# Gate slabs 2, 4 and 6 in halves over neighbouring pairs of heads, and three orders made fixed, in a two-layer decoder trunk

## The chip, the core and the metric

The kernel runs on one core of one Trainium2 chip. The time is device microseconds of one execution; the number that is compared is the median of several executions. A matrix engine (PE, with its weight loads shown apart as PEld), a vector engine (DVE), an activation engine (ACT), a general engine (POOL) and a queue engine that issues the transfers (SP) run beside each other, each through its own list of instructions in order, and wait for each other on semaphores.

## The reference

Two layers over 1024 tokens of width 1024. Each computes one input projection with the columns [main | memory queries | main gate | memory gate], then a main branch and a cross-attention of four heads into 256 memory tokens, and then the output projection and a layer norm.

```
h = x @ w_in
y = concat([main(u_main) * silu(g_main), memory(q_mem) * silu(g_mem)])
x = layer_norm(alpha * x + y @ w_out)
```

Layer 0's main branch is a causal pooling. Layer 1's is the part that the change touches, attention of 16 heads of 64 channels with forget gates; k, v and cum come from one shared projection of layer 1's input:

```
logits[t, s] = q_t . k_s / 8 + cum[t] - cum[s]      (s <= t)
out = softmax(logits) @ v
```

Everything is in float32. The kernel splits each float32 operand of a product into a high and a low part and adds three products (high·high, high·low, low·high).

## The kernel before

Nearly all matrix work comes in slabs. A slab (`slab`, L169) is 128 output channels by 1024 tokens: 48 products of 512 columns, in two weight pieces of 256 KB; for each piece come 12 products for tokens 0 to 511 and then 12 for tokens 512 to 1023. A piece is loaded through SP into a tile `raw` (4 buffers) and split into two tiles `w` (6 buffers); in the attention of layer 1 POOL does that split (`gp_hi_lo`, L144 and L145), elsewhere ACT and DVE (`hi_lo`, L140 and L141). When a 512-token half is complete it is taken out of the accumulator (`pj`, 3 banks): a gate by ACT L192 and DVE L193, keys by L645 and L646, queries by L656 and L657, values by an ACT copy (L669) and then `values_of`, which halves them to 16 bit and has them transposed by SP.

The stage of the change is `fox` (L781). It goes through the 16 heads in order, two heads to a pair, and in each head through 8 steps i = 0..7, one for each tile of 128 queries, the longest (tile 7, 1024 keys) first. A step on tile i of a head has these parts:

- `probs` (L692): POOL masks the diagonal block of the row tile R (L702); the mask of a tile writes what the previous tile's maximum read, so it follows that maximum. PE multiplies queries by keys in one or two parts of up to 512 keys (L167, into `L`, 2 banks). DVE adds R and takes the running minimum of the negated logits in one instruction for each part (L709); that frees the bank. ACT takes the exponentials into `T` with their sums (L715).
- `halves` of the tile before, called by `behind` between the last maximum and the exponentials in program order: DVE adds the sums (L726 or L728) and inverts them (L729); ACT scales to a 16-bit high half (L732), DVE gives the low half (L733).
- `turn` (L742): SP transposes both halves.
- `values` (L746), five steps later (LAG): PE multiplies by the values (L167, into `O`, 1 bank), ACT and DVE take it out into `o` (L758, L759). `pair_out` multiplies `o` by the pair's gate on POOL (L768) and stores it to y1d.

Between these, `Fill.pump` hands PE products of slabs that are needed later: the fills. Each pair of heads spreads its own fills evenly over its 16 steps, 0.4 of a step's share ahead of the values and 0.6 behind them. During pair p the fills hold the keys, queries and values of pair p+1 (three slabs, none of them in pair 7), and gates: 0 and 1 in pair 0, 2 in pair 2, 4 in pair 4, 7 in pair 7. Gates 3, 5 and 6 are fills of pair 7 too, as `late_gate`: the stored pair is read back from y1d into an `R` buffer (2 in all), multiplied on POOL (L778) and stored again. So the pairs 0 to 7 have 3, 3, 4, 3, 4, 3, 3 and 4 slabs.

In pair 7 the first 8 of 24 pieces of W_out are also loaded (`OutProj.fetch`, L350) and split on ACT and DVE (`OutProj.split`, through `hi_lo`), and two pieces of the memory branch's output (`OutProj.early`). Five more steps follow the last head (`hd == HEADS`), with the output projection's first 48 products as fill, and then `OutProj.rest`, the projection and the norm.

PE is under `manual_schedule`: its order is the program's. On the other engines and on SP a scheduler places the instructions ahead of time by its own model of when their inputs are ready, with the program order as priority, so an instruction can be placed ahead of others that come before it in the program. At run time every engine keeps the placed order.

Of the kernel before, what the change touches and what calls it, by code (L numbers as in the profile page):

```python
# [18 lines left out]
P = 128  # L19
S = 1024  # L20
# [51 lines left out]
def trunk_kernel(ctx, tc, x, xT, memT, win, wk, wv0, wv, wmk, wmv, wout, poolw, pscale, lng, lnb, bforget, out):  # L72
# [65 lines left out]
    def hi_lo(hi, lo, src):  # L138

        nc.scalar.copy(hi, src)  # L140
        nc.vector.tensor_tensor(lo, src, hi.bitcast(F32), ALU.subtract)  # L141
# [27 lines left out]
    def slab(pieces_dram, XH, XL, evac, banks=("pj", 3)):  # L169

        accs = [ps([P, NH], *banks) for _ in range(2)]
        for pc in range(2):
            ready = isinstance(pieces_dram, list)
            h, l = pieces_dram[pc] if ready else split_w(pieces_dram[pc], [P, 4, P])
            for n in range(2):
                for k in range(4):
                    kt = pc * 4 + k
                    for i, (a, b) in enumerate(((h, XH), (h, XL), (l, XH))):
                        nc.tensor.matmul(  # L179
                            accs[n], a[:, k, :], b[:, kt, n * NH : (n + 1) * NH],  # L180
                            start=kt == 0 and i == 0, stop=kt == KT - 1 and i == 2,
                        )
# [76 lines left out]
    def gate_units(w_dram, dst, XH, XL):  # L259
        return slab(w_dram, XH, XL, lambda cols, acc: gate(acc, dst[:, cols]))  # L260
# [75 lines left out]
    class OutProj:  # L336
# [16 lines left out]
        def split(self, upto):  # L353

            while self.n < upto:
                self.fetch(self.n + 1)
                n = self.n
                kk, nh, j = self.KKS[n // 4], n // 2 % 2, n % 2
                if j == 0:
                    self.ws[nh][kk] = self.wtile(n // 2)  # L360
                h, lo = self.ws[nh][kk]
                hi_lo(h[j], lo[j], self.raws.pop(0))
                self.n += 1
# [18 lines left out]
        def early(self, yh, yl):  # L382


            for j in range(2):
                r, two = raw([P, 2, 2 * P]), slice(2 * j, 2 * j + 2)
                nc.sync.dma_start(r, self.yd[2, :, two, : 2 * P])
                yield
                hi_lo(yh[:, two, :], yl[:, two, :], r)
# [146 lines left out]
    with tc.tile_pool(name="in1", bufs=1) as in1:  # L536
# [101 lines left out]
        def qk_units(p):  # L638
# [12 lines left out]
            yield from slab(wk[p], XH, XL, k_evac)  # L651
            qs = [xy() for _ in range(2)]
# [9 lines left out]
            pairs[p] = list(zip(qs, ks, ws))  # L662

        def pair_units(p):

            yield from qk_units(p)
            if p >= 2:
                u = MK([P, S], F32)
                yield from slab(wv[p - 2], XH, XL, lambda cols, acc: nc.scalar.copy(u[:, cols], acc))  # L669
            pairs[p].append(first_vs[p] if p < 2 else values_of(u))  # L670
# [15 lines left out]

        def forget_rows(hd):
# [4 lines left out]
        def probs(hd, i, R, sums, behind):  # L692
# [9 lines left out]
            nc.gpsimd.affine_select(R[:, qs], R[:, qs], [[-1, P]], ALU.is_ge, -NEG, base=0, channel_multiplier=1)  # L702
# [3 lines left out]
            for n, (lo, up) in enumerate(parts):  # L706
# [3 lines left out]
                top = m[:, n : n + 1]  # L710
            behind()
# [9 lines left out]
        def halves(hd, i, es, sums):  # L721

            L, r = (i + 1) * P, tiny(1)
            one, two = (sums[:, n, hd % 2, i : i + 1] for n in range(2))
            if len(es) == 2:
# [3 lines left out]
            nc.vector.reciprocal(r, r)  # L729
            pair = sb([P, 2 * S], "P", 4, F16)  # L730
# [50 lines left out]
        def fox(following, out_proj):  # L781
# [3 lines left out]
            def gate_ahead(pr):  # L785
                gs[pr] = G()
                fill.add(gate_units(win[1, 12 + pr], gs[pr], XH, XL), SLAB)

            ahead_R = forget_rows(0)
            for hd in range(HEADS + 1):  # L790
# [3 lines left out]
                if hd < HEADS:  # L794
                    if b == 0:
# [3 lines left out]
                        for ahead in {0: (0, 1), 2: (2,), 4: (4,), 7: (7,)}.get(pr, ()):  # L799
                            gate_ahead(ahead)  # L800
                            if ahead == 0:
                                fill.add(following, SLAB)
                        for late in (3, 5, 6) if pr == 7 else ():
                            fill.add(late_gate(late), SLAB)
                    R, ahead_R = ahead_R, None
                for i in range(ST if hd < HEADS else LAG):
# [3 lines left out]
                    new, split = None, []  # L810

# [7 lines left out]
                    if pr == 7:  # L819
                        step = b * ST + i  # L820
                        if step == 7:
                            lead = out_proj.early(*(xy((P, 4, 2 * P)) for _ in range(2)))
                        if step in (7, 9, 10, 12):
                            next(lead)
                        out_proj.split(min(step - 1, 6) if step < 14 else step - 7)
                        out_proj.fetch(min(step + 1, 6) if step < 12 else min(step - 5, 8))
                    if hd < HEADS:
                        new = (hd, tile_of, o)
                        fresh[0] = probs(hd, tile_of, R, sums, behind)
                    else:  # L830
                        behind()
                    fill.pump(part * FRAC[0])
# [82 lines left out]
```

## Time and profile before

| what | value |
|---|---|
| median of 3 runs | 1272.26 us (1271.57 to 1277.35) |
| profiled execution, its own time | 1275.16 us |
| its span, first to last instruction | 1273.4 us |
| granted PE clock, mean | 0.997 |
| DMA moved | 178.66 MB |

The profile is of one execution. Busy times are of one engine; an engine can be busy for several instructions at once, since they overlap in its pipeline. The number behind an x counts instructions. In a timeline row stand the start, the duration, engine, line and operation, out<-in by tile names, and in brackets how long the engine was idle ahead of it and on whom it waited. A row of the waits gives the total, the number of waits and the longest one.

### The profile page before, as it was taken

The page shows a single profiled execution, that of the slowest core. Times are in us where ns is not written, and L with a number is a line of the kernel's source. Part 1 is how long each engine was busy: PE and PEld are TensorE (multiplying, and loading weights), DVE is VectorE, ACT ScalarE, POOL GpSimd, SP SyncE. Part 2 cuts the span into 40 slices and gives each one's busy share as a digit, 9 for nine tenths or more (in the row PEclk, how much of TensorE's full clock was granted, in tenths as well). Part 3 has the DMA queues.
Part 4 walks back from the last instruction along what each step waited for, and adds up shares of the span by engine and source line. Part 5 has one row for each costly group of instructions (what it writes and reads, how often), then busy time and mean ns, then how long its engine had stood idle before and what let it go on. Part 6 is the DMA issues. An engine that isn't in the chain of part 4 may idle for free. (4 is left out here: it accounts for less than half of the span.)

```text
span 1273.4 us, 19681 instructions
## 1 busy us (share of the span) xinstructions
PE 1243.5 (98%) x7018; PEld 1032.7 (81%) x7018; DVE 803.8 (63%) x1901; ACT 578.5 (45%) x1273; POOL 174.2 (14%) x276
## 2 busy tenths in 40 slices
PE   9999999999999999999999999999999999899997
PEld 6888888888888888888887778887887777777885
DVE  6444766376455555377456878777877887664644
ACT  5233643242321123266225777666667677652110
POOL 0000000000000000000013334342333323430000
PEclk9999999999999999999999999999999999999999
DMA  6333444232553324244516786867877687884430
GB/s 224 108 100 100 117 117 132 83 119 89 158 197 100 106 84 134 75 116 115 162 51 180 137 184 155 195 157 175 187 160 178 157 196 171 209 224 149 166 115 34
DMA packets 267427, 178.66 MB, mean 140 GB/s; under 512 B 212288, under 2 KB 225728, under 8 KB 267328
## 3 DMA queue, kind: packets, MB, share of 16 engines
q1 hardware_dynamic: 267328, 177.40, 52.3%
q8 instruction: 55, 0.90, 0.3%
q14 instruction: 44, 0.36, 0.1%
HBM read 94.97 MB, written 22.61 MB: 92 GB/s over the span
## 5 line engine op out<-in xcount | busy, mean ns | idle before, releaser
L179 PE MATMUL pj<-A,w 128*128 128x512 f32 x2928 | 723.4, 395 | 0.8 <-ACT A L140 0.8
L179 PEld LDWEIGHTS pj<-A,w 128*128 128x128 f32 x2928 | 536.5, 188 | 103.9 <-ACT A L140 2.4
L141 DVE TENSOR_TENSOR w<-raw,w 128x512 fp32r<-128x512 f32 x106 | 74.0, 700 | 105.9 <-ACT w L140 105.1
L715 ACT ACTIVATE T<-MK,s 128x512 f32<-128x512 f32 x192 | 110.8, 577 | 53.1 <-DVE s L709 39.6
L140 ACT CAST w<-raw 128x512 fp32r<-128x512 f32 x106 | 65.7, 621 | 149.8 <-PE pj L179 103.0
L733 DVE SCALAR_TENSOR_TENSOR P<-T,s,P 128x512 f16<-128x512 f32 x192 | 111.5, 613 | 29.8 <-ACT P L732 27.6
L732 ACT ACTIVATE P<-T,s 128x512 f16<-128x512 f32 x192 | 102.7, 576 | 45.5 <-issue 17.2
L167 PE MATMUL L<-B,B 128*128 128x512 f32 (+3 forms) x384 | 92.0, 344 | 14.5 <-DVE s L709 14.1
L167 PEld LDWEIGHTS L<-B,B 128*128 128x128 f32 x384 | 69.8, 188 | 36.8 <-DVE s L709 23.9
L619 POOL MEMSET G<- 128x128 f32 x1 | 0.2, 205 | 610.2 <-DVE V L333 610.2
L709 DVE CUSTOM_DVE_ANT_0 MK<-L,R 128x512 f32<-128x512 f32 (+3 forms) x128 | 72.9, 570 | 12.0 <-PE L L167 7.2
L167 PEld LDWEIGHTS <-V 128*128 128x128 f16 x1152 | 65.2, 99 | 18.6 <-issue 18.6
L167 PE MATMUL O<-T,V 128*128 128x128 f16 x1152 | 76.2, 221 | 1.1 <-DVE G L759 1.1
L141 DVE TENSOR_TENSOR T<-T,T 128x1024 fp32r<-128x1024 f32 x23 | 28.1, 1223 | 70.2 <-PE L L376 51.3
L145 POOL TENSOR_TENSOR w<-raw,w 128x512 fp32r<-128x512 f32 x54 | 70.6, 1307 | 3.8
L140 ACT CAST T<-T 128x1024 fp32r<-128x1024 f32 x23 | 24.2, 1050 | 98.4 <-DMA T<-y0d 50.6
L702 POOL TENSOR_SCALAR_AFFINE_SELECT R<-R 128x128 f32<-128x128 f32 x128 | 42.7, 336 | 180.4 <-DVE s L709 99.2
L144 POOL TENSOR_SCALAR w<-raw 128x512 fp32r<-128x512 f32 x54 | 35.8, 664 | 139.9 <-PE pj L179 131.3
L212 PE MATMUL pj<-T,w 128*128 128x256 f32 x384 | 48.7, 284 | 0.9 <-DVE w L141 0.8
L212 PEld LDWEIGHTS pj<-T,w 128*128 128x128 f32 x384 | 47.6, 192 | 2.0 <-DVE w L141 1.3
L376 PE MATMUL pj<-B,T 128*128 128x512 f32 x186 | 46.5, 392 | 0.5 <-DVE T L141 0.5
L376 PE MATMUL L<-B,T 128*128 128x512 f32 x174 | 43.0, 391 | 0.0
(214 smaller groups left out, 1598.1 us busy)
## 6 DMA issues: line engine op xcount, KB each, us to landing
raw<-in_win_dram SPq DMA_DIRECT2D x96, 256.0 KB, 2.8
raw<-in_wout_dram SPq DMA_DIRECT2D x48, 256.0 KB, 2.9
B<-B SPq DMA_DIRECT2D x32, 256.0 KB, 4.0
R<-cumd SPq DMA_DIRECT2D x16, 512.0 KB, 4.3
y0d<-Y SPq DMA_DIRECT2D x12, 512.0 KB, 3.1
T<-y0d SPq DMA_DIRECT2D x12, 512.0 KB, 3.9
T<-y1d SPq DMA_DIRECT2D x11, 512.0 KB, 4.3
raw<-in_wmk_dram SPq DMA_DIRECT2D x16, 256.0 KB, 2.6
```

The lines of the kernel that those rows point to most:

```text
L140: nc.scalar.copy(hi, src)
L141: nc.vector.tensor_tensor(lo, src, hi.bitcast(F32), ALU.subtract)
L145: nc.gpsimd.tensor_tensor(lo, src, hi.bitcast(F32), ALU.subtract)
L167: nc.tensor.matmul(acc, a, b, start=i == 0, stop=i == len(terms) - 1)
L179: nc.tensor.matmul(accs[n], a[:, k, :], b[:, kt, n * NH : (n + 1) * NH], start=kt == 0 and i == 0, stop=kt == KT - 1 and i == 2,)
L212: nc.tensor.matmul(acc, w[:, k, :], m[pc][:, k, :], start=pc == 0 and k == 0 and i == 0, stop=pc == 1 and k == 3 and i == 2,)
L376: nc.tensor.matmul(accs[a][nh], y[:, k, a * P : (a + 1) * P], w, start=kt == 8 and i == 0, stop=kt == 7 and i == 2,)
L702: nc.gpsimd.affine_select(R[:, qs], R[:, qs], [[-1, P]], ALU.is_ge, -NEG, base=0, channel_multiplier=1)
L709: nc.vector.tensor_tensor_reduce(p[:, lo:up], lg, R[:, lo:up], 1.0, top, ALU.add, ALU.min, m[:, n : n + 1])
L715: nc.scalar.activation(e, p[:, lo:up], AF.Exp, bias=top, scale=-1.0, accum_out=sums[:, n, hd % 2, i : i + 1],)
L732: nc.scalar.activation(pair[:, lo:up], e, AF.Copy, scale=r)
L733: nc.vector.scalar_tensor_tensor(pair[:, L + lo : L + up], e, r, pair[:, lo:up], ALU.mult, ALU.subtract)
```

## The change

Five things are done.

1. `slab` and `gate_units` take `ns`, the 512-token halves that they compute. Gate pr for the pairs 2, 4 and 6 is computed as half 0 at the end of pair pr−1's fills and half 1 at the end of pair pr's. A half loads and splits both weight pieces of its gate again. Gate 1 is in halves too, both in pair 0, ahead of and behind pair 1's remaining slab. Gate 6 is no longer a late gate. The pairs 0 to 7 then have 3, 3.5, 3.5, 3.5, 3.5, 3.5, 3.5 and 3 slabs.
2. Within a pair's fills the order is keys, values, queries (before: keys, queries, values). The half gate comes behind them. `values_of` is called behind the queries.
3. `inverse_of` (the two small DVE instructions of L726 to L729) stands in the program behind the first part of the next tile's maximum, ahead of the second; `halves` keeps the rest.
4. Each mask is placed behind the mask before it on POOL (`issue_after`).
5. The splits of W_out in `fox` and of `early` are pinned behind what precedes them in the program on ACT and on DVE (`keep_in_program_order`). They stand behind `probs` of their step rather than ahead of it, and their steps and those of the loads are given by two lists. The splits in `rest` are not pinned.

```diff
     def hi_lo(hi, lo, src, pinned=False):
+        pin = tc.keep_in_program_order if pinned else lambda ins: ins
+        pin(nc.scalar.copy(hi, src))
+        pin(nc.vector.tensor_tensor(lo, src, hi.bitcast(F32), ALU.subtract))
...
-    def slab(pieces_dram, XH, XL, evac, banks=("pj", 3)):
-        accs = [ps([P, NH], *banks) for _ in range(2)]
+    def slab(pieces_dram, XH, XL, evac, banks=("pj", 3), ns=(0, 1)):
+        accs = {n: ps([P, NH], *banks) for n in ns}
...
-            for n in range(2):
+            for n in ns:
...
+            yield from slab(wk[p], XH, XL, k_evac)
+            if p >= 2:
+                u = MK([P, S], F32)
+                yield from slab(wv[p - 2], XH, XL, lambda cols, acc: nc.scalar.copy(u[:, cols], acc))
             qs = [xy() for _ in range(2)]
...
             yield from slab(win[1, p], XH, XL, q_evac)
+            pairs[p] = [*zip(qs, ks, ws), first_vs[p] if p < 2 else values_of(u)]
...
+            with tc.issue_after(masked[-1]) if masked else nullcontext():
+                masked.append(
+                    nc.gpsimd.affine_select(R[:, qs], R[:, qs], [[-1, P]], ALU.is_ge, -NEG, base=0, channel_multiplier=1).ins
+                )
...
                 top = m[:, n : n + 1]
+                if n == 0:
+                    inverse()
             behind()
...
-            def gate_ahead(pr):
-                gs[pr] = G()
-                fill.add(gate_units(win[1, 12 + pr], gs[pr], XH, XL), SLAB)
+            def gate_ahead(pr, ns):
+                if pr not in gs:
+                    gs[pr] = G()
+                fill.add(gate_units(win[1, 12 + pr], gs[pr], XH, XL, ns), len(ns) * SLAB // 2)
...
-                        for ahead in {0: (0, 1), 2: (2,), 4: (4,), 7: (7,)}.get(pr, ()):
-                            gate_ahead(ahead)
-                            if ahead == 0:
-                                fill.add(following, SLAB)
-                        for late in (3, 5, 6) if pr == 7 else ():
+                        if pr == 0:
+                            gate_ahead(0, (0, 1))
+                            gate_ahead(1, (0,))
+                            fill.add(following, SLAB)
+                            gate_ahead(1, (1,))
+                        elif pr == 7:
+                            gate_ahead(7, (0, 1))
+                        else:
+                            gate_ahead(pr + pr % 2, (1 - pr % 2,))
+                        for late in (3, 5) if pr == 7 else ():
                             fill.add(late_gate(late), SLAB)
...
                     if pr == 7:
                         step = b * ST + i
-                        if step == 7:
+                        out_proj.fetch((0, 0, 1, 2, 3, 4, 5, 6, 6, 6, 7, 7, 7, 8, 8, 8)[step])
+                        if step == 9:
                             lead = out_proj.early(*(xy((P, 4, 2 * P)) for _ in range(2)))
-                        if step in (7, 9, 10, 12):
+                        if step in (9, 12):
                             next(lead)
-                        out_proj.split(min(step - 1, 6) if step < 14 else step - 7)
-                        out_proj.fetch(min(step + 1, 6) if step < 12 else min(step - 5, 8))
...
+                    if pr == 7:
+                        out_proj.split((0, 0, 0, 1, 2, 3, 4, 5, 6, 6, 6, 6, 7, 7, 8, 8)[step], True)
+                        if step in (11, 15):
+                            next(lead)
```

More of the change, by code (lines that the diff above doesn't have):

```diff
@@ L1 @@
-from contextlib import ExitStack
+from contextlib import ExitStack, nullcontext
 from itertools import islice
@@ L257, in transposes, with gate_units @@
         since[0] = 0
-    def gate_units(w_dram, dst, XH, XL):
-        return slab(w_dram, XH, XL, lambda cols, acc: gate(acc, dst[:, cols]))
+    def gate_units(w_dram, dst, XH, XL, ns=(0, 1)):
+        return slab(w_dram, XH, XL, lambda cols, acc: gate(acc, dst[:, cols]), ns=ns)
     def mem_attention(l, XH, XL, kv, qtile, ytile, yd):
@@ L351, in fetch, with split @@
                 self.raws.append(r)
-        def split(self, upto):
+        def split(self, upto, pinned=False):
             while self.n < upto:
@@ L685, in start_units @@
             yield from islice(following, 30)
+        masked = []
         def forget_rows(hd):
@@ L690, in forget_rows, with probs @@
             return R
-        def probs(hd, i, R, sums, behind):
+        def probs(hd, i, R, sums, inverse, behind):
             q, kx, ky = pairs[hd // 2][hd % 2]
@@ L729, in halves @@
             nc.vector.reciprocal(r, r)
+            return r
+        def halves(hd, i, es, r):
+            L = (i + 1) * P
             pair = sb([P, 2 * S], "P", 4, F16)
```

31 lines of the change are left out of this document (13 added, 18 removed).

## The prediction

> **What bounds the kernel now.** I read the page first, for the engines' shares.
>
> ```profile
> span 1273.4 us, 19681 instructions
> ...
> PE 1243.5 (98%) x7018; PEld 1032.7 (81%) x7018; DVE 803.8 (63%) x1901; ACT 578.5 (45%) x1273; POOL 174.2 (14%) x276
> ```
>
> PE is busy 98% of the span, and the change takes no product away: the same slabs are computed, in another order. So only time in which PE stands, or runs slowly, can be won. Next came the windows, cut where the first query-key product of each pair of heads stands in the timeline (pairs 0 to 7, then the five last steps with the beginning of the output projection).
>
> ```profile
> core 0: us, PE busy (x) PEld busy (x) DVE busy (x) ACT busy (x) POOL busy (x), PEclk, DMA share, GB/s
> 672.70:723.40 50.70, 48.78 (x295) 39.50 (x295) 39.72 (x116) 35.27 (x85) 17.02 (x30) 1.00 0.75 167
> 723.40:776.40 53.00, 51.24 (x337) 41.58 (x337) 41.36 (x121) 37.54 (x90) 18.91 (x32) 1.00 0.75 172
> 776.40:837.60 61.20, 61.20 (x385) 50.86 (x385) 47.72 (x138) 41.67 (x95) 23.44 (x35) 1.00 0.76 175
> 837.60:890.30 52.70, 51.09 (x337) 41.60 (x337) 40.88 (x118) 37.28 (x89) 18.83 (x32) 1.00 0.74 169
> 890.30:951.60 61.30, 61.30 (x387) 50.93 (x385) 47.71 (x138) 41.66 (x95) 21.27 (x32) 1.00 0.79 171
> 951.60:1004.10 52.50, 51.07 (x337) 41.63 (x336) 40.89 (x118) 37.28 (x89) 18.83 (x32) 1.00 0.77 173
> 1004.10:1057.10 53.00, 51.37 (x337) 41.53 (x336) 43.42 (x127) 38.90 (x91) 16.94 (x28) 1.00 0.79 180
> 1057.10:1124.60 67.50, 61.39 (x374) 49.46 (x372) 48.44 (x133) 43.14 (x98) 25.37 (x36) 0.97 0.83 195
> 1124.60:1155.80 31.20, 28.57 (x154) 22.32 (x152) 19.17 (x28) 13.73 (x24) 7.64 (x8) 1.00 0.79 259
> ```
>
> The columns are length, then busy time of PE, PEld, DVE, ACT and POOL. Pairs 2 and 4, with four slabs, are full: PE is busy from end to end. The three-slab pairs 1, 3, 5 and 6 are not. What a slab costs is seen where PE runs undisturbed, in the chain of waits:
>
> ```profile
> 1166.59 5.44 PE pj L376 x24
> ```
>
> 24 products of 512 columns take 5.44 us, so a slab of 48 takes 10.9. A four-slab pair is longer by only 61.25 − 52.8 = 8.45 us. The lighter pairs thus lose 2.4 us each, and pair 7, with four slabs and 67.5 us, loses over 6. The waits say of whom:
>
> ```profile
> PE L L167 <- DVE s L709: 14.1, 15, 3.1
> POOL R L702 <- DMA R<-cumd: 45.2, 11, 8.8
> DVE P L733 <- ACT P L732: 27.6, 58, 1.1
> DVE s L726 <- ACT T L715: 21.6, 18, 4.9
> POOL w L144 <- PE pj L179: 131.3, 37, 47.8
> ```
>
> PE stands 14.1 us in all for a bank of logits that the maximum (L709) has not read yet. The timeline of pair 1's second head shows why the maximum is late there:
>
> ```profile
> 756.22 0.73 PE L167 MATMUL L<-B,B 128*128 128x512 f32 x2 [0.22 <-DVE s L709]
> 757.41 0.51 PE L167 MATMUL L<-B,B 128*128 128x256 f32 x2 [0.46 <-DVE s L709]
> 759.02 0.54 POOL L702 TENSOR_SCALAR_AFFINE_SELECT R<-R 128x128 f32<-128x128 f32 x2 [6.66 <-DMA R<-cumd]
> 759.60 0.48 DVE L709 CUSTOM_DVE_ANT_0 MK<-L,R,s 128x256 f32<-128x256 f32 x1 [0.80 <-POOL R L702]
> 764.59 0.73 PE L167 MATMUL L<-B,B 128*128 128x512 f32 x2 [1.08 <-DVE s L709]
> ```
>
> POOL holds two masks. The first is the next head's and waits 6.66 us for its row to land; the second is the one that the running head needs, queued behind it. When it comes, DVE has stood 0.80 us, and PE stands 0.22 + 0.46 + 1.08 = 1.76 us. In pair 7 it is something else:
>
> ```profile
> 1076.03 0.73 PE L167 MATMUL L<-B,B 128*128 128x512 f32 x2 [2.39 <-DVE s L709]
> ...
> 1097.89 2.81 POOL L778 TENSOR_TENSOR R<-R,G 128x256 f32<-128x256 f32 x4 [4.92 <-DMA R<-y1d]
> 1098.41 1.32 ACT L140 CAST B<-raw 128x512 fp32r<-128x512 f32 x2 [3.87 <-DMA raw<-in_wout_dram]
> 1101.18 0.21 DVE L726 TENSOR_SCALAR s<-sums 128x1 f32<-128x1 f32 x1 [4.88 <-ACT T L715]
> 1102.82 0.73 PE L167 MATMUL L<-B,B 128*128 128x512 f32 x2 [3.11 <-DVE s L709]
> ...
> 1104.90:1108.40 3.50, 3.50 (x20) 2.73 (x19) 2.65 (x9) 2.35 (x6) 1.59 (x3) 0.51 0.99 212
> ```
>
> Two W_out casts stand ahead of the exponentials on ACT and wait 3.87 us for their pieces; four products of a late gate stand ahead of a mask on POOL. DVE then waits 4.88 us for the sums and PE 3.11. The last row, a window, shows the granted clock at 0.51 for 3.5 us just after: another 1.7 us lost.
>
> **The change part by part.** *Half gates, the order of masks, pairs 1 to 6.* Today these six take 53.0 + 61.2 + 52.7 + 61.3 + 52.5 + 53.0 = 333.7 us with 20 slabs. After, they hold 21, gate 6's slab coming from pair 7, so like for like today is 333.7 + 10.9 = 344.6. Two roads give the length of a pair with 3.5 slabs. From a full one, half a slab less: 61.25 − 5.44 = 55.8. From a light one, without the mask's stall, half a slab more: 52.8 − 1.76 + 5.44 = 56.5. I take 56.1: 336.6, a gain of 8.0 us. The ends are 55.8 (gain 9.8) and a pair that goes on losing what the light ones lose, 52.8 + 5.44 = 58.24 (loss 4.8). DVE's 47.7 busy us in a full pair, 41 to 43 in a light one, fit under 56.
>
> *What the halves add.* Eight more weight pieces to load and to split on POOL; away go one read and one store of 512 KB, and four products L778, for which four L768 come.
>
> ```profile
> L145 POOL TENSOR_TENSOR w<-raw,w 128x512 fp32r<-128x512 f32 x54 | 70.6, 1307 | 3.8
> L144 POOL TENSOR_SCALAR w<-raw 128x512 fp32r<-128x512 f32 x54 | 35.8, 664 | 139.9 <-PE pj L179 131.3 <-DMA raw<-in_win_dram 8.5
> ```
>
> A split is 0.66 + 1.31 = 1.97 us, so POOL gets 15.8 us more over six pairs, where it is busy 17 to 23 of 53 to 61. In a half slab each piece feeds 12 products, 2.72 us at the least, and POOL mostly waits for PE to free a buffer (131.3 us). I cost it at nothing; if a late transfer holds POOL, a mask or PE's weights come late by that wait, at most what the 4.92 us shows.
>
> *Queries last.* The next pair's first product needs them. Their last half is complete 24 products ahead of the pair's end, 5.4 us with other steps' products between, and is taken out by two of these on DVE behind two on ACT:
>
> ```profile
> L657 DVE SCALAR_TENSOR_TENSOR B<-pj,B 64x512 fp32r<-64x512 f32 x32 | 22.0, 689 | 2.2 <-ACT B L656 1.3
> ```
>
> That is some 2 us on each engine, and the half gate covers it. Without that cover each pair would begin up to 2 us late. The values' raw tile is kept through the queries' slab: one of four `MK` buffers, of which the maxima need two at a time. Both at nothing.
>
> *The inverse inside the maximum.* It lets ACT begin the high half one part (0.6 us) sooner; today DVE waits 27.6 us for ACT's L732, 58 times. Against it: the 18 waits for the sums (21.6 us, 1.2 each) may come to stand ahead of the second part, and behind them wait that part, the bank that it frees and PE. For pairs 1 to 6 both ends lie within those above; I add nothing there.
>
> *Pair 7.* It gives a slab away: 67.5 − 10.9 = 56.6 like for like. If the pinned casts and the ordered masks end the stalls, 3.11 + 2.39 + 1.7 = 7.2 us go: 49.4. DVE doesn't allow that:
>
> ```profile
> L193 DVE SCALAR_TENSOR_TENSOR G<-G,pj 128x512 f32<-128x512 f32 x32 | 21.9, 684 | 7.1 <-ACT G L192 6.3
> raw<-in_wout_dram SPq DMA_DIRECT2D x8, 256.0 KB, 4.1
> ```
>
> Its 48.4 busy us lose one gate, 2 × 0.68, and are 47.0. In the last light pair DVE was not busy for 53.0 − 43.4 = 9.6 us, 1.8 of them the mask's stall: 47.0 + 7.8 = 54.8. The earlier inverse takes at most 27.6 / 8 = 3.4 us of that: 51.4. I take the middle, 53.1, a gain of 3.5; the ends are none and 7.2. The pins add a wait that the trace does not show: a pinned cast stops ACT until its piece has landed, and behind it stand the next high half, the values' first copy and the next exponentials; on DVE the pinned difference holds the low half and the next maximum. A piece is asked for in a step and cast behind the exponentials of the next one, 3.3 us (53 / 16) or more later; it lands after 4.1 us in the median of pair 7 (the second row). So short waits are likely and long ones are not; up to 1 us each hides in ACT's idle time (42 busy of 53).
>
> [...]
>
> *The five last steps.* `rest` keeps its unpinned splits. PE is idle 31.2 − 28.6 = 2.6 us there; I take no change, and ±2.6 as ends.
>
> *The sum.* 8.0 + 3.5 = 11.5 us less. The profiled execution took 1275.16 us (span 1273.4 and what lies around it) and would take 1263.7; the median of the three runs lies 2.9 us lower, so the forecast is 1272.26 − 11.5 = 1260.8. Its own range is 1252.7 (9.8 + 7.2 + 2.6 less) to 1265.9.
>
> **The rivals.** *DVE becomes the bound in every pair.* The inverse's waits land inside the maximum and pairs 1 to 6 stay as lossy as light ones: +4.8 − 3.5 = +1.3, so 1273.6, no change. For it: DVE at 41 to 43 of 53 us. Against it: pairs 2 and 4 ran full with the same work on DVE per head. 0.12.
>
> *The pinned casts stop ACT (slower).* Ten casts in pair 7 with a wait of w each take 10w, of which 11 us hide in ACT's idle time. From w = 2.3 us this eats the whole gain; at 3 us, below the 3.87 seen above, it costs 30 − 11 = 19 us: 1279.8. For it: 4.1 us to land against a step of 3.3, on a queue that also issues the transposes in order. Against it: the casts come a step later than the loads. 0.13.
>
> *POOL and DVE hold each other up.* Some rows of the same operation:
>
> ```profile
> L141 DVE TENSOR_TENSOR B<-raw,B 128x512 fp32r<-128x512 f32 x6 | 5.6, 949 | 0.0
> L141 DVE TENSOR_TENSOR w<-raw,w 128x512 fp32r<-128x512 f32 x106 | 74.0, 700 | 105.9 <-ACT w L140 105.1
> ```
>
> The first is of pair 7, with POOL at work, and takes 949 ns instead of 700. If the eight new splits held DVE for half of their 15.8 us, 7.9 of the 11.5 would go: 1268.7, no change. Against it: L657 and L193, which read one operand from an accumulator, keep 689 and 684 ns in the same stage. 0.06. [...]
>
> *It doesn't do what it says in pair 7.* A pin fixes only what precedes a cast in the program, and late gates 3 and 5 still read through R. Pair 7 wins nothing: 1272.26 − 8.0 = 1264.3. 0.11.
>
> **How the numbers follow.** The forecast has the remaining 0.58. A measurement of this kernel can tell about 0.5% from no change: 6.4 us, so faster is below 1265.9 and slower above 1278.6. Faster: 0.57 + 0.10 of the last rival = 0.67. Slower: 0.13 of the casts and 0.02 for their mixture with the others = 0.15. The rest, 0.18, is no change. The range goes from the forecast's low end, 1252.7, up over the DVE rival to 1274.0; it leaves out the casts' case and a little on either side, under 0.2.
>
> **What would show it.** Right: the masks' wait for R (45.2 us, 11 times) nearly gone, with none queued ahead of a running head's; pairs 1 to 6 at 56 us each with PE idle under 0.5; pair 7 near 53 without a window at half clock; PE's 14.1 us for L709 below 5. Wrong: pairs at 58, with L726 ahead of a second L709 in DVE's waits; or ACT's casts waiting over 2 us for W_out in pair 7 with PE standing behind L709; or L141 and L247 stretched beside L145.

## The result, and the profile after

| | before | after |
|---|---|---|
| median of 8 runs | 1276.15 us (1271.57 to 1281.69) | 1283.06 us (1279.83 to 1285.36) |
| profiled execution, its span | 1273.4 us | 1280.5 us |

The ratio is 1.0048 (95% interval 1.0029 to 1.0067): slower by half a per cent, where 11.5 us less was forecast. From the page of the changed kernel:

```profile
span 1280.5 us, 19721 instructions
...
PE 1245.0 (97%) x7018; PEld 1036.3 (81%) x7018; DVE 808.1 (63%) x1901; ACT 580.3 (45%) x1273; POOL 185.3 (14%) x292
```

The work is the same and the shares have hardly moved; the stages tell more. Windows of the changed kernel, cut at the same products as before (pairs 0 to 7, the last steps, and two short stretches of pair 7); the last three columns are the granted clock, the DMA share and GB/s:

```profile
core 0: us, PE busy (x) PEld busy (x) DVE busy (x) ACT busy (x) POOL busy (x), PEclk, DMA share, GB/s
671.40:721.00 49.60, 48.25 (x295) 39.69 (x295) 38.70 (x115) 34.55 (x83) 20.63 (x34) 1.00 0.74 175
721.00:777.50 56.50, 56.14 (x362) 46.37 (x362) 43.77 (x123) 39.71 (x92) 22.28 (x37) 1.00 0.75 170
777.50:835.00 57.50, 56.28 (x361) 46.20 (x360) 44.90 (x129) 39.55 (x92) 23.07 (x36) 1.00 0.88 175
835.00:892.30 57.30, 56.13 (x362) 46.36 (x361) 45.45 (x129) 39.78 (x92) 23.19 (x37) 1.00 0.86 175
...
1006.80:1063.90 57.10, 56.04 (x361) 46.33 (x360) 45.29 (x129) 39.78 (x92) 20.21 (x32) 1.00 0.79 176
1063.90:1132.20 68.30, 54.92 (x327) 43.14 (x327) 45.72 (x131) 41.54 (x98) 18.38 (x31) 0.88 0.72 171
1132.20:1163.40 31.20, 27.97 (x153) 22.36 (x152) 19.34 (x29) 13.86 (x25) 8.23 (x8) 1.00 0.78 243
1088.40:1095.20 6.80, 6.09 (x28) 4.74 (x28) 3.72 (x9) 2.46 (x6) 1.45 (x3) 0.50 1.05 211
1119.10:1129.40 10.30, 5.42 (x14) 3.60 (x15) 3.81 (x12) 5.06 (x13) 2.18 (x3) 0.50 0.84 200
```

Pairs 1 to 6 run from 721.0 to 1063.9, 342.9 us, where 344.6 was the like-for-like time before: they win 1.7 us instead of 8.0. From the second on each has PE idle for about 1.2 us. Pair 7 holds a slab less and still takes 68.3 us, 11.7 above the 56.6 of like for like; PE stands 13.4 us in it (68.30 − 54.92), and 17.1 us of it, the last two rows, are at half clock. With 1.3 us less ahead of pair 0, 1.1 less in it and 0.5 less behind pair 7 the sum is −1.3 − 1.1 − 1.7 + 11.7 − 0.5 = +7.1 us, the difference of the spans.

PE's waits in the two stages, then two of DVE's:

```profile
PE pj L180 <- POOL w L145: 11.2, 2, 6.8
PE L L168 <- DVE s L710: 4.4, 7, 1.2
PE L L168 <- DVE s L730: 4.4, 4, 1.2
...
DVE P L740 <- ACT P L739: 32.0, 49, 1.7
DVE s L728 <- ACT T L718: 28.0, 33, 1.6
```

The lines have moved by one or more (L710 is the maximum, L145 the high half of a weight split, L730 the sum that stands behind the maximum). The 14.1 us of waits for the maximum are down to 4.4, as forecast, and no mask waits for its R any more. New are two waits for POOL's weights, and one wait of 1.06 to 1.17 us at the start of each of the pairs 2 to 7 (four of these six are in the row of L730, two in that of L710). Single rows of the timeline show both. First the end of pair 2 and the start of pair 3:

```profile
833.50 1.29 POOL L146 TENSOR_TENSOR w<-raw,w 128x512 fp32r<-128x512 f32 x1
833.55 2.32 DVE L248 SCALAR_TENSOR_TENSOR MK<-MK,s,MK 128x1024 f16<-128x1024 f32 x1
836.43 0.28 DVE L710 CUSTOM_DVE_ANT_0 MK<-L,R 128x128 f32<-128x128 f32 x1
836.78 0.51 PE L168 MATMUL L<-B,B 128*128 128x512 f32 x1 [1.17 <-DVE s L730]
```

L248 is the values' low half in `values_of`, L146 the split of a weight piece of the half gate. DVE starts 55 ns behind POOL and takes 2.32 us; the old pair's last maximum (L710, 128 keys) is queued behind it, and PE, whose next product needs a bank of logits, stands 1.17 us. Then pair 7:

```profile
1063.65 0.33 SPq L351 DMA_DIRECT2D raw<-in_wout_dram  x1
...
1071.03 12.17 SPq L749 DMA_TRANSPOSE T<-P  x4
1082.60 0.60 ACT L141 CAST MK<-raw 128x512 fp32r<-128x512 f32 x1
1083.23 0.69 DVE L142 TENSOR_TENSOR MK<-raw,MK 128x512 fp32r<-128x512 f32 x1
1083.95 0.33 SPq L150 DMA_DIRECT2D raw<-in_win_dram  x1
1086.76 1.06 POOL L145 TENSOR_SCALAR w<-raw 128x512 fp32r<-128x512 f32 x1
...
1117.35 0.69 DVE L142 TENSOR_TENSOR B<-raw,B 128x512 fp32r<-128x512 f32 x1
1118.18 0.42 SPq L150 DMA_DIRECT2D raw<-in_win_dram  x1
1123.18 0.62 POOL L145 TENSOR_SCALAR w<-raw 128x512 fp32r<-128x512 f32 x1 [4.99 <-DMA raw<-in_win_dram]
1123.85 0.79 PE L180 MATMUL pj<-A,w 128*128 128x512 f32 x1 [6.76 <-POOL w L145]
```

A gate's weight load (L150) is issued 0.03 us after a pinned split (L142, of W_out or of the memory branch's pieces) has ended, and later another one 0.14 us after a second such split: no `raw` buffer was free before. The rows of SP, ACT and DVE tell who held them. Four W_out pieces were asked for (L351) at 1040.89, 1051.65, 1058.56 and 1063.65 us, all ahead of pair 7, since the change pins the splits but not the loads, and the scheduler had placed the loads earlier; the first of these pieces was cast (L141) at 1082.60. So from 1063.65 to 1083.92 us all four buffers held W_out pieces, and from 1106.89 to 1118.04 pieces of W_out and of the memory branch. The four transposes ahead of the first load did not fill SP's queue: in 6.4 of their 12.17 us SP waited for the low halves. The weights then reach PE 4.41 and 6.76 us too late. The first window at half clock begins 0.5 us behind the first wait, the second one inside the second wait.

### The profile page after: what moved, and what is told of

Same layout as the page of the kernel before. It is cut to its first block, busy times and chain, and to the rows that moved or that the text cites. A ratio compares the mean times of both kernels' runs of the same rounds, so it can differ in the third digit from the quotient of the medians.

```text
span 1280.5 us, 19721 instructions
## 1 busy us (share of the span) xinstructions
PE 1245.0 (97%) x7018; PEld 1036.3 (81%) x7018; DVE 808.1 (63%) x1901; ACT 580.3 (45%) x1273; POOL 185.3 (14%) x292
## 5 line engine op out<-in xcount | busy, mean ns | idle before, releaser
L180 PE MATMUL pj<-A,w 128*128 128x512 f32 x2928 | 727.9, 396 | 12.5 <-POOL w L145 11.2
L142 DVE TENSOR_TENSOR w<-raw,w 128x512 fp32r<-128x512 f32 x106 | 73.5, 695 | 106.6 <-ACT w L141 105.8
L740 DVE SCALAR_TENSOR_TENSOR P<-T,s,P 128x512 f16<-128x512 f32 x192 | 113.0, 614 | 34.1 <-ACT P L739 32.0
L141 ACT CAST w<-raw 128x512 fp32r<-128x512 f32 x106 | 65.7, 621 | 150.8 <-PE pj L180 104.1
L710 DVE CUSTOM_DVE_ANT_0 MK<-L,R 128x512 f32<-128x512 f32 (+3 forms) x128 | 73.0, 570 | 16.5 <-PE L L168 13.3
L146 POOL TENSOR_TENSOR w<-raw,w 128x512 fp32r<-128x512 f32 x62 | 79.9, 1289 | 6.5 <-PE pj L180 2.9
L142 DVE TENSOR_TENSOR T<-T,T 128x1024 fp32r<-128x1024 f32 x23 | 28.1, 1224 | 68.1 <-PE L L377 49.9
L141 ACT CAST T<-T 128x1024 fp32r<-128x1024 f32 x23 | 24.2, 1051 | 98.3 <-DMA T<-y0d 50.1
L145 POOL TENSOR_SCALAR w<-raw 128x512 fp32r<-128x512 f32 x62 | 42.3, 683 | 151.3 <-PE pj L180 93.3
L702 POOL TENSOR_SCALAR_AFFINE_SELECT R<-R 128x128 f32<-128x128 f32 x128 | 37.1, 296 | 151.6 <-DVE s L710 92.9
```

What stands on the lines that cost most here:

```text
L141: pin(nc.scalar.copy(hi, src))
L142: pin(nc.vector.tensor_tensor(lo, src, hi.bitcast(F32), ALU.subtract))
L145: nc.gpsimd.tensor_scalar(hi, src, 1.0, 1.0, ALU.mult, ALU.mult)
L146: nc.gpsimd.tensor_tensor(lo, src, hi.bitcast(F32), ALU.subtract)
L180: nc.tensor.matmul(accs[n], a[:, k, :], b[:, kt, n * NH : (n + 1) * NH], start=kt == 0 and i == 0, stop=kt == KT - 1 and i == 2,)
L710: nc.vector.tensor_tensor_reduce(p[:, lo:up], lg, R[:, lo:up], 1.0, top, ALU.add, ALU.min, m[:, n : n + 1])
```

## Experiments

Three theories for pair 7. *Ring* (A in what was written ahead of the runs): the four `raw` buffers are held by W_out and memory pieces until their pinned splits run, and the gates' loads, which feed PE at once, wait for a buffer. *Too short* (B): with a slab less, pair 7 is too short for all that SP issues in it. *Pins*: a pinned cast stops ACT or DVE for a piece that has not landed, as the prediction's slower rival had it. Three for pairs 1 to 6. *Meeting* (C): the half gate puts a POOL split beside the values' low half, which takes 2.32 us instead of 1.28. *Inverse* (D): the inverse, ahead of the second part of the maximum, holds up the bank that PE waits for. *Halves*: a pair with a half gate simply costs more on its engines.

Behind a median stand its ratio to the kernel before, timed along with it (medians of 1275.89 to 1277.38 us), and the 95% interval of that ratio.

**e1: part 5 undone.** The old steps for the loads and splits, and no pins.

```diff
-                        out_proj.fetch((0, 0, 1, 2, 3, 4, 5, 6, 6, 6, 7, 7, 7, 8, 8, 8)[step])
+                        out_proj.split(min(step - 1, 6) if step < 14 else step - 7)
+                        out_proj.fetch(min(step + 1, 6) if step < 12 else min(step - 5, 8))
...
-                        out_proj.split((0, 0, 0, 1, 2, 3, 4, 5, 6, 6, 6, 6, 7, 7, 8, 8)[step], True)
```

> The changed kernel with its part 5 undone: W_out and the memory branch's pieces are loaded and split in the steps of the kernel before, without pins. Theory A (the ring): in pair 7 the gates' weight loads wait for a raw buffer that a pinned split has not released, PE runs dry behind POOL's L145 (11.2 us in two waits) and then at half clock. Then PE's waits for POOL w fall under 1 us, pair 7 goes from 68.3 us to 54 to 58 and the whole from about 1283 to 1269 to 1273. Theory B (pair 7 has become too short with three slabs for what SP issues in it): PE still waits 5 us or more for POOL w, pair 7 stays over 64 and the time over 1278. Pairs 1 to 6 stay at 57.2 us under both.

1271.76 us, 0.9968 (0.9956 to 0.9980). The window of its pair 7:

```profile
1064.70:1120.20 55.50, 50.31 (x327) 39.32 (x326) 44.77 (x128) 39.71 (x95) 19.27 (x31) 1.00 0.85 207
```

55.5 instead of 68.3 us at full clock, and the waits for POOL's weights are gone, with all ten pieces still loaded in a pair with three slabs: *too short* falls. Part 5 is the loss in pair 7. In return PE waits there for the maximum again, 5.1 us in six waits where the changed kernel has 1.4 in two. Pairs 2 to 6 stayed at 57.1 to 58.4 us.

**e2: pins without loads.** The ten pinned splits read a resident tile; their ten loads are left out, so that part of the output projection is computed from other numbers.

```diff
             while self.n < upto:
+                if pinned:
+                    self.raws.append(XH[:, 0, :NH].bitcast(F32))
...
-                        out_proj.fetch((0, 0, 1, 2, 3, 4, 5, 6, 6, 6, 7, 7, 7, 8, 8, 8)[step])
```

> The changed kernel with the pins, but in pair 7 the ten pinned splits read a resident tile: the eight W_out pieces and the two pieces of the memory branch are not loaded there (part of the output projection is computed from other numbers), so no pinned split holds a raw buffer. Theory A (the ring): PE's waits for POOL w are gone, pair 7 at 53 to 57 us, no window at half clock in it. A pinned cast that stops ACT by itself, as the prediction's slower rival had it with the wait on its load: ACT has no load to wait for, so this run can't show that wait, but if the pins' places alone were the cost, pair 7 stays over 62. Theory B (too short a pair): some relief by ten loads fewer, but at least one wait of over 2 us for POOL w stays.

1269.49 us in a single execution. Pair 7:

```profile
1065.90:1116.80 50.90, 49.31 (x327) 39.59 (x326) 41.99 (x125) 37.78 (x91) 20.38 (x31) 1.00 0.82 166
```

With the pins in place and no piece in the ring, pair 7 is at its shortest, 2 us below what was expected: *ring*, not the order of the casts on ACT. Since this kernel moves ten pieces less, its 50.9 us are a lower end rather than the price of pins alone, and since its casts have no load to wait for, it can't judge *pins*. The changed kernel's own trace does: in its pair 7 ACT's casts wait for W_out twice, 4.4 us in all, and PE stands behind the maximum for 0.3, beside the 1.1 at the pair's start.

**e6: part 5 without its pins.** The lists of steps stay.

```diff
-                        out_proj.split((0, 0, 0, 1, 2, 3, 4, 5, 6, 6, 6, 6, 7, 7, 8, 8)[step], True)
+                        out_proj.split((0, 0, 0, 1, 2, 3, 4, 5, 6, 6, 6, 6, 7, 7, 8, 8)[step])
...
```

> The changed kernel with its lists of steps for W_out kept, but no pins. Which half of part 5 fills the ring: if the pins (a raw buffer stays taken until ACT and DVE come to the pinned split), then PE's waits for POOL w fall below 2 us, pair 7 lasts 55 to 58 us and the whole 1270 to 1274; if the lists (loads asked for too early take buffers from the gates), the waits stay over 5 us and the whole over 1278.

1278.17 us, 1.0008 (0.9993 to 1.0024), outside what was expected. The waits for POOL's weights are gone and pair 7 takes 59.5 us. But what the pins were for is back; two timeline rows:

```profile
1078.79 0.62 ACT L141 CAST B<-raw 128x512 fp32r<-128x512 f32 x1 [4.56 <-DMA raw<-in_wout_dram]
1081.45 0.50 PE L168 MATMUL L<-B,B 128*128 128x256 f32 x2 [2.80 <-DVE s L710]
```

A cast floats ahead and stops ACT for 4.56 us. So the pins hold the ring: unpinned, the first W_out split of pair 7 ends at 1068.3 us, 2.6 us behind the fourth load, and not 20.3. Without them the old stall comes back, and PE waits for the maximum 14.7 us in all.

**e7: pins with the pieces spread.** One piece every two steps, so that fewer buffers are held at a time, and the memory pieces from steps 4 and 10.

```diff
-                        out_proj.fetch((0, 0, 1, 2, 3, 4, 5, 6, 6, 6, 7, 7, 7, 8, 8, 8)[step])
+                        out_proj.fetch(step // 2 + 1)
...
-                        out_proj.split((0, 0, 0, 1, 2, 3, 4, 5, 6, 6, 6, 6, 7, 7, 8, 8)[step], True)
+                        out_proj.split((step + 1) // 2, True)
```

> The changed kernel with its pins, but with other lists of steps: W_out pieces evenly, one each two steps, asked for in an even step and split at the end of the next; the memory branch's two pieces in steps 4 to 5 and 10 to 11. So a pinned split holds one raw buffer (two in four of 16 steps) and not two or more. Theory A (the ring): with two or three buffers left to the gates PE waits for POOL w under 2 us in pair 7, which lasts 52 to 56 us with the 1.2 us at its beginning; whole 1267 to 1272. If pins cost as such, whatever is held: over 1276.

1276.34 us, 0.9990 (0.9979 to 1.0000). PE's wait for L145 in pair 7 fell from 11.2 to 2.5 us and pair 7 to 57.2, both short of what *ring* expected. The whole did not follow: from the end of pair 7 to PE's last product it takes 142.5 us, 139.2 in the changed kernel. Pair 7 gave 11.1 us and 3.3 came back behind it. The time is where the rival put it (pins that cost something as such, over 1276); yet in this pair 7 no pinned cast waits for a load, and PE waits 3.1 us for weights and 2.4 for the maximum, 1.1 of this at the pair's start.

**e3: part 1 undone.** Whole gates in pairs 0, 2, 4 and 7 and three late gates, all else as changed.

```diff
-                            gate_ahead(pr + pr % 2, (1 - pr % 2,))
-                        for late in (3, 5) if pr == 7 else ():
+                        for ahead in {0: (0, 1), 2: (2,), 4: (4,), 7: (7,)}.get(pr, ()):
+                            gate_ahead(ahead, (0, 1))
...
+                        for late in (3, 5, 6) if pr == 7 else ():
```

> The changed kernel with its part 1 undone: gates 2 and 4 whole, gate 6 a late gate of pair 7; the masks' order, queries last, the inverse and the pins are kept. Theory C (port): the values' low half (L248 in the changed kernel) takes 2.32 us instead of 1.28 in six pairs since POOL's L146 splits the half gate's weights just then, and the next pair's second tile stalls 1.2 us. Without half gates behind the values the instruction is back at 1.28 us at least in pairs 1, 3, 5 and 6, and these pairs last 50.5 to 51.5 us, 2 and 4 61 us. Theory D (the inverse ahead of the second part of the maximum delays the bank that PE waits for): the 1.2 us at the pairs' beginnings stay, and the light pairs last 52 or more. Pair 7 with four slabs and the pins: theory A has PE dry again for several us, 72 to 79 us; theory B (too short a pair) says 62 to 65 us. Whole: 1272 to 1280 by A and C.

1286.02 us, 1.0093 (1.0068 to 1.0117), outside what was expected. L248 is back at 1.28 us in pairs 1, 3, 5 and 6, as *meeting* had it (in pairs 2 and 4, where it starts 0.4 us behind a split of the whole gate, it takes 1.95), but another wait took its place, and these four pairs last 53.6 to 54.4 us. PE's longest waits, and a row of its timeline:

```profile
PE L L168 <- DVE B L661: 9.0, 4, 2.9
PE pj L180 <- POOL w L145: 7.2, 2, 3.9
```

```profile
776.53 1.20 PE L168 MATMUL L<-B,B 128*128 128x512 f32 x4 [2.05 <-DVE B L661]
```

Where a pair ends with the queries (pairs 1, 3, 5 and 6), the next one's first product waits 2.05 to 2.88 us until they are taken out. Part 2 needs the cover of part 1. It means that this run does not separate *meeting* from *inverse* or *halves*. Its pair 7, with four slabs and the pins, takes 73.4 us and has PE waiting for POOL's weights, as *ring* had it.

**e4: values taken out earlier.** `values_of` behind the values' slab, ahead of the queries' slab; the half gates stay.

```diff
                 yield from slab(wv[p - 2], XH, XL, lambda cols, acc: nc.scalar.copy(u[:, cols], acc))
+                vs = values_of(u)
             qs = [xy() for _ in range(2)]
...
-            pairs[p] = [*zip(qs, ks, ws), first_vs[p] if p < 2 else values_of(u)]
+            pairs[p] = [*zip(qs, ks, ws), first_vs[p] if p < 2 else vs]
```

> The changed kernel with values_of called ahead of the queries' slab and not behind it, so that the halving of the values falls in the middle of a pair. Theory C (port): where L248 doesn't meet a POOL split it takes 1.28 us, the 1.2 us at the beginnings of pairs 2 to 7 go, and pairs 1 to 6 last 56 us each: about 6 us less, 1277. If it meets the split of the queries' weights, it stays at 2.3 us but in another place. Theory D (inverse): the wait at the pairs' beginnings stays, 1283.

1274.10 us, 0.9985 (0.9969 to 1.0001), 9.0 us below the changed kernel's median. The group of L248 by shape (count | busy, mean ns | idle before), in the changed kernel, then here, and a window of a pair here:

```profile
L248 DVE SCALAR_TENSOR_TENSOR MK<-MK,s,MK 128x1024 f16<-128x1024 f32 x8 | 16.5, 2058 | 0.6
```

```profile
L248 DVE SCALAR_TENSOR_TENSOR MK<-MK,s,MK 128x1024 f16<-128x1024 f32 x8 | 10.2, 1280 | 0.0
```

```profile
835.80:891.60 55.80, 55.80 (x362) 46.39 (x361) 44.11 (x128) 39.96 (x93) 23.63 (x36) 1.00 0.83 180
```

The same low halves take 1.28 us again and the pairs 3 to 6 are full, PE busy 55.80 of 55.80. Pairs 1 to 6 together take 336.1 us instead of 342.9. *Meeting* holds; *inverse* falls, since the inverse is where it was, and so does *halves*: a half gate costs no more than its products. Beside each of these six low halves a mask now starts on POOL, some 0.15 us behind it; it is the mask that takes 1.28 us instead of 0.29, and in all six pairs PE waits for the maximum 0.8 us. Pair 7 keeps the ring's waits, 10.6 us in two, and takes 64.1 us.

**e5: the masks' order alone**, put on the kernel before.

```diff
-            nc.gpsimd.affine_select(R[:, qs], R[:, qs], [[-1, P]], ALU.is_ge, -NEG, base=0, channel_multiplier=1)
+            with tc.issue_after(masked[-1]) if masked else nullcontext():
+                masked.append(
...
```

> The kernel before with the masks' order alone. The prediction's reading: the next head's mask ahead of the running one's costs PE 1.76 us in each of pairs 1, 3, 5 and 6; with the order these go to 51 us and the whole is 5 to 7 us shorter, about 1269. Rival: DVE was late there for another reason (the queries taken out just then), and the mask's wait is a by-product; e3 kept 0.42 and 0.63 us of PE's loss at that place with the masks in order. Then pairs 1, 3, 5 and 6 stay over 52 us and the whole changes by less than 2 us.

1273.13 us, 0.9979 (0.9966 to 0.9993). The masks' wait for R to land falls from 45.2 us in 11 waits to 1.5 in one, and the light pairs 1, 3, 5 and 6 take 52.4, 52.1, 52.1 and 53.0 us instead of 53.0, 52.7, 52.5 and 53.0. That is half a microsecond, not the 1.76 that the prediction gave the stall: of the three waits that it added up, 0.22, 0.46 and 1.08 us, the first two stay (0.24 and 0.46) and the third falls to 0.46. These pairs stay over 52 us, as the rival had it. The whole is 3.1 us below the median of the kernel before, between the two expectations; the six pairs give 1.8 of it, and 0.9 in the profiled executions lie ahead of pair 0, where nothing was changed.

**c1: both remedies**, e1 with e4's edit. **c2**: c1 with `inverse()` moved behind the maximum's loop, undoing part 3:

```diff
-                if n == 0:
-                    inverse()
+            inverse()
             behind()
```

> The changed kernel with part 5 undone and values_of called ahead of the queries' slab: both remedies together. Theories A and C, each seen alone, should add: pairs 1 to 6 at 55.8 to 56.5 us (e4), pair 7 at 54 to 55.5 us without PE waiting for POOL w (e1, less the 1.3 us at its beginning), 1262 to 1266 us. If they don't add (the casts that are free to float collide with the values' halving moved forward), 1268 to 1272.

> As c1, with the inverse of the sums put back behind both parts of the maximum. The prediction's step: inside the maximum it saves up to 3.4 us of DVE's waits for ACT in pair 7 and nothing in pairs 1 to 6, which PE bounds at 55.8. Then this is 1 to 4 us slower than c1, all of it in pair 7 and the five last steps. Theory D (the inverse ahead of the second part holds up the bank): this is 1 to 4 us faster than c1.

1268.68 us, 0.9938 (0.9922 to 0.9955), and 1267.13 us, 0.9933 (0.9915 to 0.9952). Pairs 3 to 6 are at 55.8 to 56.0 us in both. The two remedies do not add: pair 7 takes 58.0 and 57.7 us, for a floating cast stops ACT, and so DVE and PE. Two rows of c2, and a window behind them that shows half clock:

```profile
1067.44 0.62 ACT L141 CAST B<-raw 128x512 fp32r<-128x512 f32 x1 [3.68 <-DMA raw<-in_wout_dram]
1070.02 0.80 PE L168 MATMUL L<-B,B 128*128 128x256 f32 x2 [4.22 <-DVE s L711]
```

```profile
1070.00:1073.40 3.40, 3.38 (x16) 2.67 (x17) 3.35 (x10) 1.78 (x6) 1.15 (x3) 0.50 0.63 148
```

The place of the inverse makes no difference that can be told.

**c3: the best version.** c2 with e7's pinned, spread pieces. **c5**: c3 with the inverse inside the maximum, which is all five parts of the change with the two remedies. **c4**: c3 with the splits of `rest` pinned too. The edits of c3 and c5 are those of e7 and c2 (undone); that of c4:

```diff
         def rest(self, resid, XH, XL, dst):
-            self.split(24)
+            self.split(24, True)
```

> e7 with the values' halving ahead of the queries and the inverse behind the maximum, as in c2. The parts add: pairs 1 to 6 at 55.8, pair 7 at 50.5 to 54, where c2 had 57.7 with 4.2 us of PE behind a cast that had floated ahead of its load; whole 1259 to 1264, the fastest so far. If the pins bring ACT's waits for loads instead (a piece lands 4.1 us after it is asked for and has two steps, 6.4 us), pair 7 stays at 57 and the whole at 1267.

> c3 with the inverse inside the maximum again: all five parts of the change, with two remedies (the values' halving ahead of the queries, W_out in one piece each two steps). It asks what the inverse's place is worth once the two causes are gone. The prediction gave it up to 3.4 us in pair 7: then 1262 to 1265, and pair 7 at 53 to 55. c1 against c2 showed no gain (0.9938 and 0.9933): then 1265 to 1269, the same as c3 within its interval, with pair 7 at 55 to 56.5.

> c3 with the splits of the rest of W_out pinned as well. In the five last steps of all versions a cast that has floated ahead of the values' copy (L765) waits for its load and PE stands 1.1 to 3.3 us for the O bank. Pinned, that wait goes: 2 to 4 us less than c3. Rival: the projection's first products then come too soon for their weights, since the splits can't begin before the last values are out: 5 us or more slower than c3.

c3 took 1266.54 us (1264.14 to 1269.66), 0.9912 (0.9894 to 0.9930); c5 1266.56, 0.9918 (0.9901 to 0.9934); c4 1267.84, 0.9914 (0.9897 to 0.9932). Pair 7 of c3, PE's longest waits in c3, and the one that c4 has instead:

```profile
1056.60:1112.10 55.50, 51.86 (x327) 41.63 (x326) 38.84 (x111) 35.30 (x84) 18.40 (x30) 0.94 0.77 173
```

```profile
PE O L168 <- DVE G L766: 3.8, 2, 3.3
PE pj L180 <- POOL w L145: 2.6, 1, 2.6
```

```profile
PE pj L377 <- ACT B L141: 2.8, 1, 2.8
```

c3 is 10.8 us below the kernel before, close to the 11.5 forecast for the change, by other steps. It missed what was expected of it (1259 to 1264, pair 7 at most 54), though none of its pinned casts in pair 7 waits for a load. The pair 7 of c5 takes 56.1 us, as expected. c5 says that part 3 is worth nothing here. In c4 the wait for the `O` bank behind floating W_out casts falls from 3.8 to 0.5 us, and the projection's products wait 2.8 us for their weights instead: the wait moved, and neither of c4's two expectations came.

## Why the prediction was wrong

**Pairs 1 to 6: the mechanism was right, one cost at nothing was not.** The step that failed is "What the halves add … I cost it at nothing". The split on POOL was weighed as POOL's time and found to wait for PE; what counts is which DVE instruction stands beside it. Six of the eight 1024-wide low halves meet it and take 2.32 instead of 1.28 us, and PE stands 1.06 to 1.17 us at the start of the pairs 2 to 7. With POOL no longer ahead of the low half (e4) the six pairs take 336.1 us against the 336.6 forecast, and the window is 55.8, the first road's figure (a full pair less half a slab). The second road stood on the masks' stall of 1.76 us, and e5 shows it worth about 0.5, since two of its three waits had nothing to do with the mask: 52.8 − 0.5 + 5.44 = 57.7. So the two roads agreed by luck, and 56.1 is near the truth because of the first.

**The rival "POOL and DVE hold each other up" had the mechanism and the wrong victim.** It spread half of the splits' 15.8 us over DVE at large and got 7.9 us; e4 got back 9.0 us in the medians, 6.8 of it in these pairs. It was given 0.06, on the ground that L657 and L193 keep their times beside POOL. Those read one operand from an accumulator. So do two that kept their times in the changed kernel's trace too: the queries' take-out L661 at 0.69 us, beside a running L146 and with POOL idle, and the low half L740 at 0.75 us for 512 keys, in both cases. The two that were stretched, the difference of a W_out piece (L141, the prediction's 949 ns, and 1.71 us in one that ran beside L145) and the values' low half (L248), read both operands from SBUF tiles. The search should have been for a DVE instruction of that kind that the new order puts beside a split: L247 (L248 after) is named in the last part of the prediction, and it is the one. Beside a POOL instruction of 1.29 us it lost 1.04 us.

**Pair 7: the wait was looked for in the wrong queue.** The step that failed is "The pins add a wait": it priced the time that a cast waits for its piece and found it hidden in ACT's idle time. Its premise, "A piece is asked for in a step and cast behind the exponentials of the next one", did not hold for loads that are not pinned: the first piece was asked for at 1040.89 us, in pair 6, and cast at 1082.60, 41.7 us later rather than some 3.3. The cost lies before the cast. A piece that waits for its pinned place holds one of four buffers, and the gates' loads can't be issued until it is free. The 4.92 us bound ("if a late transfer holds POOL, … PE's weights come late by that wait") was at the right place but stood under the halves; 4.41 and 6.76 us were measured, and half clock in 17.1 us on top, with 6.09 + 5.42 us of PE work in it at half speed, another 5.8. Together 4.41 + 0.71 (one more wait, for L146) + 6.76 + 5.8 = 17.7 us: without them pair 7 would be at 50.6, and e2, where no piece is in the ring, shows 50.9. Whether the 53.1 of the forecast can be had with the pieces loaded stays open: the best that does so, c4, has 54.7. The slower rival gave the right sign with the wrong mechanism (ACT stopped by pinned casts): in the changed kernel's pair 7 PE stood 1.4 us behind the maximum, 1.1 of it from the meeting, and 11.2 us for the weights of L145.

**What held.** The masks no longer wait for R. PE's waits for the maximum fell from 14.1 to 4.4 us, and 2.2 of these 4.4 are of the meeting. Gate 6's slab fits into pairs 1 to 6. The queries' take-out costs about 2 us without its cover: 2.05 to 2.88 us in e3. The inverse is worth nothing in pairs 1 to 6; nor is it in pair 7, where up to 3.4 us was allowed (c1 against c2, c5 against c3), and DVE's 27.6 us of waits for ACT's high half became 32.0.

**Open.** In c3 and c5 one gate load in pair 7 is still 2.5 to 2.6 us late. Every shorter pair 7 was followed by a longer end: 139.2 us in the changed kernel from pair 7 to PE's last product, 140.5 in e1, 142.0 in c3, 142.5 in e7. The `O` bank's wait is part of it; c4 moved that without a gain, and the rest was not tried. What the three-slab pairs of the kernel before lose beside the masks was not found either; pairs of three and a half slabs do not lose it (e4).

## What to carry to other kernels

When a step is pinned, ask what it holds while it waits (a buffer, a bank), since when (its load may not be pinned with it), and who else takes from that ring: here the harm fell on the neighbour's loads, not on the pinned instruction. When work on POOL is moved, list the DVE instructions with both operands in SBUF that then run beside it (here L248, 2.32 us instead of 1.28), and ask which of them heads a queue that PE is about to need. And when an estimate has two roads, test the assumption of each by itself: agreement between them is no evidence.

## What the runs showed of the hardware

The size of the meeting was not expected: a DVE instruction of 1.28 us that starts 51 to 55 ns behind a POOL one of 1.29 us takes 2.32 us, nearly one after the other; all six took 2.32 us and the other two 1.28. The one that started first kept its time: of the two at 1.28 us one began 0.26 us ahead of a POOL split, and there it was POOL's instruction (L145) that took 1.51 us instead of 0.62.

The clock after a wait was not a matter of its length alone. A wait of 2.60 us (c3, pair 7) was followed by a granted clock of 0.50 over 6.80 us and one of 2.11 us (e4, behind pair 7) by 0.59 over 3.80 us, but waits of 2.05 us (e3) and 3.21 us (e1) by 1.00:

```profile
1086.20:1093.00 6.80, 6.01 (x30) 4.48 (x31) 1.21 (x5) 2.22 (x6) 2.22 (x4) 0.50 0.81 202
```

```profile
1137.60:1141.00 3.40, 2.58 (x14) 1.62 (x13) 1.62 (x2) 2.67 (x5) 0.73 (x1) 1.00 0.84 272
```

The first row is the window behind c3's wait, the second that behind e1's. In the traces of the kernel before and of the changed one the changes of the granted clock lie on a grid of 3.41 us: the stretches at half clock inside the kernel last 3.41 us before, 6.83 and 10.24 us after, which are one, two and three cells, and the two after begin 30.72 us apart, nine cells. Cut on that grid, the last cell at full clock ahead of such a stretch has PE idle for 1.70 us (before), 2.87 and 2.05 us (after, in the two waits for L145). No other cell at full clock up to PE's last product has more than 1.87 us, which is more than 1.70, so no single figure parts the two kinds here. In c3 and e4 the windows put the start of half clock at about 1086.1 and 1139.9 us; the 3.41 us ahead of it hold about 2.5 and 2.1 us of PE's idle time. In e3 a later stretch at half clock begins at about 1062.2 us, and the same grid, laid from there, cuts the wait of 2.05 us into about 1.0 and 1.1. For e1's wait no window shows where a cell would end. Since 2 to 3 us of idle time within one cell stood ahead of half clock in four of these cases, a wait of over 2 us is best priced with the halved clock behind it as a possibility.
